# A hybrid attention and convolution layer: a convolution branch is moved beside the attention, its weights are kept in DRAM, and its norm runs in float32r

## The chip, the cores and the metric

The kernel runs on one core of a Trainium2 chip. The metric is the time of one execution on the device in microseconds (us). The time before is the median of three runs, 3138.69 us (3136.90 to 3145.14).

A core has a matrix engine (TensorE, PE in the profile; PEld is its loading of weights), a vector engine (VectorE, DVE), an activation engine (ScalarE, ACT), GpSimd (POOL) and SyncE (SP), which here issues all transfers. Each engine works through its own queue in order and waits for the others by semaphores.

## The reference

One layer over a sequence of 2048 tokens of width 1024, in float32. The input is normalised and projected by one matrix to nine blocks of 1024 columns. One branch is a stick-breaking attention with 16 heads of 64, one a causal convolution of 31 taps for each channel with a layer norm over the channels. Each branch has a gate inside, a projection, and a gate for the sum.

```python
h = x @ w_in
q, k, v, z_sb, c_val, c_gate, z_cv, g_sb, g_cv = jnp.split(h, SPLIT_POINTS, axis=-1)
o_sb = _stick_breaking_attention(to_heads(q), to_heads(k), to_heads(v)).reshape(bsz, seq, SB_WIDTH)
y_sb = (o_sb * jax.nn.silu(z_sb)) @ w_sb_proj
u = c_val * jax.nn.sigmoid(c_gate)
u = _causal_depthwise_conv(u, conv_w, conv_b)          # 31 taps per channel
u = jax.nn.silu(_layer_norm(u, conv_ln_g, conv_ln_b))
y_cv = (u * jax.nn.silu(z_cv)) @ w_cv_proj
merged = jax.nn.sigmoid(g_sb) * y_sb + jax.nn.sigmoid(g_cv) * y_cv
return _layer_norm(DEEPNORM_ALPHA * x + merged @ w_out, ln_g, ln_b)
```

## The kernel before

**Tiling.** Activations lie with channels on the 128 partitions. The sequence is reversed and cut into four chunks c of 512 tokens, and two halves h of 1024: half 1 (chunks 3 and 2) holds the earliest tokens, half 0 (chunks 1 and 0) the later ones. A matrix has eight blocks m of 128 rows. Every float32 product is made of three float32r products: a tensor is cut into a high and a low part by `split` (a copy on ACT, a subtraction on VectorE), and the matrix engine adds high x high, high x low and low x high. A projection block for one chunk is then 24 matmuls of 128x512 in one PSUM bank, in four pieces of six (`Fill.parts`, L201).

**Stages.** 1. First phase: the input projections by a scheme with seven instead of eight block products (L909), half 1 first, then a part of half 0. The convolution goes beside it. 2. Attention: eight pairs of heads for half 1, then for half 0. A head computes scores (`lg`, L583 and L584), a sigmoid on ACT (`nb`, L586), a scan on VectorE (L589), transposes (`tp`, L612), a split into `th` and `tl` (L117), and the products with the values (`pv`, L628). 3. End: what is left of the branches, the output product (`output`, L1243) and the last norm.

**What sets the order.** TensorE's instructions run in the order in which the program issues them. Other work for TensorE during the attention is a list of pieces, `F.pieces`: the k, q, v and z projections of half 0, then the branch projections s (after the attention) and c (after the convolution) of half 1. The list is dealt out over the attention by place: each pair of heads has a stretch of the list (`spans`, with SPLIT for half 1's share), and the list's last END places are left for after the attention. A piece without matmuls counts as a place too. On the other engines a scheduler orders by priority and data.

**The convolution** of a channel block and a half is a generator, `conv_steps`, of some 50 steps, most of them one tap on VectorE (L409). `slow_step` is called after each piece and adds PACES[phase] to a credit; with a credit of 1 or more it does one step:

```python
def slow_step(now=False):
    marks.append(newest())
    pace[0] += PACES[phase[0]]
    if not now and (not slow or pace[0] < 1):
        pace[0] = min(pace[0], 1.0)
        return
    pace[0] -= 1
    ...
        while slow and next(slow[0], slow) is slow:
            slow.pop(0)
```

The inner loop passes over generators that are used up and stops at the first step done. `u` in the first phase is the group that makes the convolution's input for one block.

**The norm of the convolution** goes by items: `conv_mean` sums over channels by a matmul with ones, then `conv_ln` for each chunk subtracts the mean and squares (s2, L467 to L474), sums the squares by matmuls with one column of ones (m2, L483), spreads the factor (m3, L494), and applies norm, gain and gates (s3, L501 to L505). Between them stand empty items, W1 or W0 in number, so that TensorE does not meet a matmul before its data. Items are set among the pieces by F.delay and F.soon (every N1 pieces for half 0).

**Branches.** `branch(n, h)` projects; its eviction multiplies by a gate (L712). The second branch of a half adds the first one's result (`other`, L714). `load_w` loads a weight block of 512 KB and splits it, unless its halves lie in DRAM already (`wdr`; so far only for some blocks of w_in). `loads` brings activations back from DRAM and splits them. Before, half 1 takes s then c beside the attention; in the end stage s of half 0, outputs of chunks 3 and 2, c of half 0, outputs 1 and 0.

**Buffers.** "st" tiles (128x512) are seven, shared by evictions, loads and the norm. mm has two PSUM banks.

Of the kernel before, what the change touches and what calls it, by code (L numbers as in the profile page):

```python
# [8 lines left out]
F32 = mybir.dt.float32  # L9
# [20 lines left out]
LAG = 3  # L30
PACES = [0.78, 1.25, 0.6]
I0 = 1
SPLIT = 0.27
RD = 9
W1 = 5
END = 14
W0 = 3
N1 = 2
O0 = 25
# [15 lines left out]
def layer_kernel(ctx: ExitStack, tc, x, w_in, w_sb, w_cv, w_out, vecs, cw, rows, out):  # L55
# [14 lines left out]
    ones = const.tile([P, P], F32, name="ones")  # L70
    nc.gpsimd.memset(ones, 1.0 / D)
    vec = const.tile([P, 5, KB], F32, name="vec")
    g_in, b_in, c_b, c_g, c_lb = (vec[:, i, :] for i in range(5))
# [70 lines left out]
    def load_w(src, col):  # L144


        hi, lo = (wp.tile([P, KB, P], F32R, name="w4", bufs=4) for _ in range(2))
        for g in range(2):
            ks = slice(g * 4, g * 4 + 4)
            if (id(src), col, g) in wdr:  # L150
                for t, e in ((hi, 0), (lo, 1)):
                    dma(t[:, ks], wdr[id(src), col, g][:, e])
                continue
            raw = wp.tile([P, 4, P], F32, name="wraw", bufs=2)
            nc.sync.dma_start(out=raw, in_=src[col // P][:, ks])
            split(raw, hi[:, ks], lo[:, ks])
        return hi, lo

# [281 lines left out]
    def conv_mean(h):  # L440

        def mean(c):
            while len(convs) < (2 - h) * KB:
                slow_step(True)
            ps, mu, ys = mm_p.tile([P, CH], F32, name="mm"), st(), st()
            dma(ys.rearrange("p (e n) -> p e n", e=2), ysd[h][:, :, c % 2 * 256:c % 2 * 256 + 256])
            nc.tensor.matmul(ps, lhsT=ones, rhs=ys, start=True, stop=True)
            nc.scalar.activation(mu, ps, AF.Copy)
            dma(mud[c], mu)
        return [lambda c=c: mean(c) for c in half(h)]  # L450

    def conv_ln(c):
# [11 lines left out]
        def s2(m):  # L464
# [5 lines left out]
            if m == 0:  # L470
                box["sq"] = sg_p.tile([P, CH], F32, name="sum", bufs=1)
                nc.vector.tensor_copy(out=box["sq"], in_=y)
            else:
                nc.vector.tensor_tensor(out=box["sq"], in0=box["sq"], in1=y, op=ALU.add)  # L474

        def m1():
# [3 lines left out]
        def m2():  # L480
            ps = mm_p.tile([P, CH], F32, name="mm")
            for b in range(nb):
                nc.tensor.matmul(ps[:, b:b + 1], lhsT=box["sq"][:, b * P:(b + 1) * P], rhs=ones[:, 0:1], start=True, stop=True)  # L483
            v = sm.tile([P, nb], F32, name="var", bufs=2)
            nc.vector.tensor_copy(out=v, in_=ps[:, :nb])
            rsqrt_eps(v, v, nb)
            box["v"] = v

        def m3():
            ps = mm_p.tile([P, CH], F32, name="mm")  # L490
            rb = st()
            nc.vector.tensor_copy(out=rb.rearrange("p (b r) -> p b r", b=nb), in_=box["v"].unsqueeze(2).to_broadcast([P, nb, P]))
            for b in range(nb):
                nc.tensor.matmul(ps[:, b * P:(b + 1) * P], lhsT=rb[:, b * P:(b + 1) * P], rhs=ident, start=True, stop=True)  # L494
            box["rs"] = copied(ps)

        def s3(m):
# [10 lines left out]
        wait = [lambda: None] * (W1 if h else W0)  # L508
        return ([m1] + wait + [(lambda m=m: s2(m)) for m in range(KB)] + wait + [m2] + wait + [m3]
                + [(lambda m=m: s3(m)) for m in range(KB)])  # L510
# [182 lines left out]
    def branch(n, h):  # L693

        def gate(m):
            def load(c):
# [20 lines left out]

        src, bys = (w_sb, [gate]) if n == "s" else (w_cv, [gate, other])
        return [(src, m * P, [(c, lambda c=c: acts[n, c]) for c in half(h)], use(m)) + tuple(b(m) for b in bys)
# [21 lines left out]
    def first_phase(F, x2, w1, ps_p):  # L741
# [257 lines left out]
        def order(h):  # L999
            us_ = [("u", m) for m in range(KB)]  # L1000
            rest = [(e, m) for m in range(4) for e in ("kqvzcgh" if h else "cgh")]
            out_ = []
            for n, u in enumerate(us_):
                out_.append(u)
                out_ += rest[len(rest) * n // 8:len(rest) * (n + 1) // 8]
            return out_

# [140 lines left out]
    with ExitStack() as s2:  # L1148
# [9 lines left out]
        for i in range(NPAIR):  # L1158
            ready[1, i] = True
        norm = conv_mean(1) + conv_ln(3) + conv_ln(2)  # L1160
        for i in range(NPAIR):
            fill_qkv(F, 0, i)
            if i < NPAIR - 2:
                F.block(*gate_z(i))
            for q in range(10):
                if norm and i >= I0:
                    F.delay(1 + 3 * q, 0.1, norm.pop(0))
        F.pair(gate_z(NPAIR - 2), gate_z(NPAIR - 1), freed=loads("s", 1))
        F.soon([(0.1, it) for it in norm], 1, 2)
        run(F, branch("s", 1), loads("c", 1))  # L1170
        F.soon([(0.1, it) for it in conv_mean(0) + conv_ln(1) + conv_ln(0)], N0, N1)
        run(F, branch("c", 1), loads("s", 0))
        end = len(F.pieces) - END
# [28 lines left out]
    with ExitStack() as s2:  # L1202
# [74 lines left out]
        run(F, branch("s", 0), loads("m", 1))  # L1277
        output(F, 3, loads("c", 0)[0])
        output(F, 2, loads("c", 0)[1])
        run(F, branch("c", 0), loads("m", 0))  # L1280
        output(F, 1, ())
# [36 lines left out]
```

## Time and profile before

| | us |
|---|---|
| median of three runs | 3138.69 |
| the profiled execution, its own time | 3146.49 |
| its span in the trace | 3144.7 |
| TensorE busy | 2896.8 |
| VectorE busy | 2603.8 |
| ScalarE busy | 1414.0 |
| first score matmul (L583) starts | 1204.0 |
| last product with the values (L628) ends | 2741.3 |

The profile is of one execution. Its numbers are read in three ways here: busy time of each engine in a stretch, with the clock that the throttle granted TensorE; idle time of an engine by what ended it ("PE tp L612 <- DVE nb L589" is the matrix engine that waited at line 612 for a tile that VectorE wrote at line 589; us in total, times, longest); and groups of like instructions. Matmuls are pipelined, so the duration of one is longer than its step from the last.

### The profile page before, as it was taken

What the parts mean: (1) busy time and instruction counts of PE and PEld (TensorE: products, weight loads), DVE (VectorE), ACT (ScalarE), POOL (GpSimd) and SP (SyncE); (2) the same over time, 40 slices, a digit from 0 to 9 for tenths busy, and PEclk for the clock granted to TensorE, in tenths of its full rate; (3) what the DMA queues carried; (4) which work ended last, traced back from release to release, by engine and by line L of the source; (5) the groups of instructions that cost most, each with busy time, mean ns of one, the idle gap of its engine ahead of it and who ended that gap; (6) DMA issues with size and microseconds to landing.
All of it is one profiled execution on the core that took longest, in us unless ns stands there. A gap on an engine that the chain in (4) does not pass through costs nothing.

```text
span 3144.7 us, 42164 instructions
## 1 busy us (share of the span) xinstructions
PE 2896.8 (92%) x14666; PEld 2402.7 (76%) x14666; DVE 2603.8 (83%) x3537; ACT 1414.0 (45%) x2582; POOL 75.4 (2%) x162
## 2 busy tenths in 40 slices
PE   6998999999999998899889889998899888879998
PEld 4776787878788886787777778887788777767887
DVE  8988989888777865998999988888988898856746
ACT  6553444444422323444454554555645555543322
POOL 1000000000000000000000000000000000000000
PEclk8999999999999999999999999999999999989999
DMA  5878757577865567555563454444543553486552
GB/s 179 301 232 307 264 194 267 206 264 282 286 222 185 176 228 218 169 182 176 182 185 119 149 172 134 156 146 140 167 129 118 158 180 120 145 288 231 169 187 81
DMA packets 319269, 604.98 MB, mean 192 GB/s; under 512 B 37456, under 2 KB 79568, under 8 KB 318928
## 3 DMA queue, kind: packets, MB, share of 16 engines
q1 hardware_dynamic: 319056, 602.29, 58.3%
q8 instruction: 115, 1.88, 0.3%
q14 instruction: 98, 0.80, 0.1%
HBM read 355.74 MB, written 246.42 MB: 191 GB/s over the span
## 4 chain that ended last, share of the span: by engine, by line
PE 47%; DVE 25%; issue 12%; DMA 7%; ACT 3%; SPq 1%; POOL 1%; DVEq 0%; POOLq 0%; ACTq 0%
PE pb L909 11%; PE mm L201 10%; DVE nb L589 10%; PE pp L909 7%; PE mm L909 7%; DVE tl L117 4%; PE tp L612 4%; PE pv L628 3%; PE lg L583 1%; DVE cy L409 1%; PE lg L584 1%; ACT th L116 1%; DVE cu L409 1%; ACT nb L586 1%; DMA st<-fdr 1%
## 5 line engine op out<-in xcount | busy, mean ns | idle before, releaser
L116 ACT ACTIVATE th<-tp 128x512 fp32r<-128x512 f32 (+1 forms) x576 | 329.6, 573 | 467.8 <-PE tp L612 459.2
L117 DVE TENSOR_TENSOR tl<-tp,th 128x512 fp32r<-128x512 f32 (+1 forms) x576 | 374.2, 652 | 92.2 <-ACT th L116 89.1
L612 PE MATMUL tp<-ident,nb 128*128 128x128 f32 x2176 | 354.6, 279 | 80.4 <-DVE nb L589 63.5
L586 ACT ACTIVATE nb<-lg 128x512 f32<-128x512 f32 (+3 forms) x640 | 331.3, 532 | 115.7 <-PE lg L584 114.0
L589 DVE TENSOR_TENSOR_SCAN nb<-nb,dd 128x256 f32<-128x256 f32 (+7 forms) x256 | 343.8, 1348 | 18.0 <-ACT nb L586 18.0
L628 PE MATMUL pv<-tl,v 128*128 128x256 f32 (+1 forms) x1152 | 303.1, 292 | 53.2 <-DVE tl L117 52.5
L612 PEld LDWEIGHTS tp<-ident,nb 128*128 128x128 f32 x2176 | 255.2, 142 | 116.7 <-DVE nb L589 78.8
L589 DVE TENSOR_TENSOR_SCAN nb<-nb,zero 128x1024 f32<-128x1024 f32 x128 | 300.1, 2347 | 23.3 <-ACT nb L586 23.1
L628 PE MATMUL pv<-th,v 128*128 128x256 f32 (+1 forms) x1152 | 307.8, 285 | 2.8 <-ACT th L116 2.6
L583 PE MATMUL lg<-k,qd 128*128 128x512 f32 (+3 forms) x640 | 267.9, 420 | 23.7 <-ACT nb L586 11.7
L628 PEld LDWEIGHTS pv<-tl,v 128*128 128x128 f32 x1152 | 219.1, 190 | 91.7 <-DVE tl L117 76.4
L628 PEld LDWEIGHTS pv<-th,v 128*128 128x128 f32 x1152 | 219.7, 191 | 20.5 <-ACT th L116 4.5
L584 PE MATMUL lg<-k,ql 128*128 128x512 f32 (+3 forms) x640 | 234.7, 367 | 0.0
L201 PE MATMUL mm<-A11h,w 128*128 128x512 f32 x512 | 185.6, 409 | 12.7 <-ACT w L116 7.0
L409 DVE SCALAR_TENSOR_TENSOR cy<-cu,csum,cy 128x512 f32<-128x512 f32 x240 | 179.2, 747 | 18.9 <-ACT cy L405 15.8
L201 PE MATMUL mm<-A12h,w 128*128 128x512 f32 x512 | 188.0, 413 | 0.0
L201 PE MATMUL mm<-SXh,w 128*128 128x512 f32 x512 | 182.8, 403 | 2.1 <-DVE st L712 2.1
L201 PE MATMUL mm<-A22h,w 128*128 128x512 f32 x512 | 182.7, 403 | 0.0
L409 DVE SCALAR_TENSOR_TENSOR cu<-cd,cwt,cu 128x512 f32<-128x512 f32 x240 | 179.1, 746 | 3.7
L409 DVE SCALAR_TENSOR_TENSOR cy<-cu,cwt,cy 128x512 f32<-128x512 f32 x240 | 179.1, 746 | 2.6
L583 PEld LDWEIGHTS lg<-k,qd 128*128 128x128 f32 x640 | 122.5, 191 | 48.7 <-ACT nb L586 29.0
L584 PEld LDWEIGHTS lg<-k,ql 128*128 128x128 f32 x640 | 123.7, 193 | 8.8 <-issue 0.2
(251 smaller groups left out, 6298.9 us busy)
## 6 DMA issues: line engine op xcount, KB each, us to landing
wdr<-w4x SPq DMA_DIRECT2D x78, 512.0 KB, 3.4
wdr<-w SPq DMA_DIRECT2D x68, 512.0 KB, 3.2
w4x<-wdr SPq DMA_DIRECT2D x52, 512.0 KB, 4.7
wraw<-in_w_in SPq DMA_DIRECT2D x100, 256.0 KB, 3.5
w<-wdr SPq DMA_DIRECT2D x96, 256.0 KB, 3.8
k<-kdr SPq DMA_DIRECT2D x192, 128.0 KB, 3.0
v<-vdr SPq DMA_DIRECT2D x96, 256.0 KB, 3.0
w<-wdr SPq DMA_DIRECT2D x46, 512.0 KB, 4.4
```

The lines of the kernel that those rows point to most:

```text
L116: nc.scalar.activation(hi, src, AF.Copy)
L117: nc.vector.tensor_tensor(out=lo, in0=src, in1=hi.bitcast(F32), op=ALU.subtract)
L201: nc.tensor.matmul(box["ps"], lhsT=l[:, kb], rhs=r[kb], start=(kb == 0 and n == 0), stop=(kb == KB - 1 and n == 2))
L409: nc.vector.scalar_tensor_tensor(out=dst, in0=src[:, j:j + HN], scalar=t, in1=first, op0=ALU.mult, op1=ALU.add)
L583: nc.tensor.matmul(lg[:, :w], lhsT=qd[c][:, js], rhs=k2[kc][:, ko:ko + w], start=True, stop=False)
L584: nc.tensor.matmul(lg[:, :w], lhsT=ql[c][:, js], rhs=k2[kc][:, ko:ko + w], start=False, stop=True)
L586: nc.scalar.activation(nb[:, o:o + w], lg[:, :w], AF.Sigmoid, scale=-QS)
L589: nc.vector.tensor_tensor_scan(out=nb[:, :w], data0=nb[:, :w], data1=dd[:, :w] if diag else zero.to_broadcast([P, w]), initial=0.0 if diag ...
L612: nc.tensor.transpose(out=tp[:, at_:at_ + P], in_=tiles[j][:, so:so + P], identity=ident)
L628: nc.tensor.matmul(o[:, :w], lhsT=lv, rhs=tt[:, o0:o0 + w], start=(diag and t == 0 and n == 0 and e == 0), stop=(last and t == nt - 1 and ...
L909: nc.tensor.matmul(bank, lhsT=wt[:, e, kb], rhs=xs_[kb][a], start=start and kb == 0 and n == 0, stop=kb == 3 and n == 2, skip_group_check= ...
```

## The change

1. The pace of the convolution in the second part of the first phase goes from 1.25 to 1.6, and the order of groups has the u groups earlier.
2. Branch c of half 0 moves from the end stage into the list beside the attention, behind branch c of half 1. It is then the first branch of its half, so s of half 0 adds its result. The norm of half 0 begins before branch s of half 1, with an item at every piece instead of every second (N1). END is 20 instead of 14.
3. `load_w` writes the split halves of w_sb and w_cv to DRAM when they are made for half 1 and reads them for half 0.
4. The norm's sums run on float32r halves (`onesr`), with two empty-item spacings changed, and the spreading of the factor is a transpose.

```diff
-PACES = [0.78, 1.25, 0.6]
+PACES = [0.78, 1.6, 0.6]
-END = 14
+END = 20
-N1 = 2
+N1 = 1
...
+    onesr = const.tile([P, P], F32R, name="onesr")
+    nc.scalar.activation(onesr, ones, AF.Copy)
...
             split(raw, hi[:, ks], lo[:, ks])
+            if src is not w_in:
+                d = wdr[id(src), col, g] = dram([P, 2, 4, P], F32R, f"wdr{len(wdr)}b")
+                dma(d[:, 0], hi[:, ks])
+                dma(d[:, 1], lo[:, ks])
...
-        def mean(c):
+        parts = {}
+
+        def prepare():
             while len(convs) < (2 - h) * KB:
                 slow_step(True)
-            ps, mu, ys = mm_p.tile([P, CH], F32, name="mm"), st(), st()
-            dma(ys.rearrange("p (e n) -> p e n", e=2), ysd[h][:, :, c % 2 * 256:c % 2 * 256 + 256])
-            nc.tensor.matmul(ps, lhsT=ones, rhs=ys, start=True, stop=True)
+            for c in half(h):
+                ys = st()
+                dma(ys.rearrange("p (e n) -> p e n", e=2), ysd[h][:, :, c % 2 * 256:c % 2 * 256 + 256])
+                parts[c] = st(F32R), st(F32R)
+                split(ys, *(t if len(ys.shape) == 2 else t.rearrange("p (e n) -> p e n", e=2) for t in parts[c]))
+
+        def mean(c):
+            ps, mu = mm_p.tile([P, CH], F32, name="mm"), st()
+            for n, t in enumerate(parts.pop(c)):
+                nc.tensor.matmul(ps, lhsT=onesr, rhs=t, start=n == 0, stop=n == 1)
...
-        return [lambda c=c: mean(c) for c in half(h)]
+        return [prepare] + [lambda: None] * W1 + [lambda c=c: mean(c) for c in half(h)]
...
+            if m == KB - 1:
+                box["sp"] = st(F32R), st(F32R)
+                split(box["sq"], *box["sp"])
...
-                nc.tensor.matmul(ps[:, b:b + 1], lhsT=box["sq"][:, b * P:(b + 1) * P], rhs=ones[:, 0:1], start=True, stop=True)
+                for n, t in enumerate(box["sp"]):
+                    nc.tensor.matmul(ps[:, 2 * b:2 * b + 2], lhsT=t[:, b * P:(b + 1) * P], rhs=onesr[:, 0:2], start=n == 0, stop=n == 1)
...
-        src, bys = (w_sb, [gate]) if n == "s" else (w_cv, [gate, other])
+        src, bys = w_sb if n == "s" else w_cv, [gate] if n == "sc"[h == 0] else [gate, other]
...
+            n = 3 if h else 1
             out_ = []
-            for n, u in enumerate(us_):
-                out_.append(u)
-                out_ += rest[len(rest) * n // 8:len(rest) * (n + 1) // 8]
-            return out_
+            for m in range(KB):
+                out_ += [("u", m)] + rest[m * n:m * n + n]
+            return out_ + rest[KB * n:]
...
-        F.soon([(0.1, it) for it in norm], 1, 2)
+        F.soon([(0.1, it) for it in slots], 1, 2)
+        F.soon([(0.1, it) for it in conv_mean(0) + conv_ln(1) + conv_ln(0)], N0, N1)
         run(F, branch("s", 1), loads("c", 1))
-        F.soon([(0.1, it) for it in conv_mean(0) + conv_ln(1) + conv_ln(0)], N0, N1)
-        run(F, branch("c", 1), loads("s", 0))
+        run(F, branch("c", 1), loads("c", 0))
+        run(F, branch("c", 0), loads("s", 0))
...
         run(F, branch("s", 0), loads("m", 1))
-        output(F, 3, loads("c", 0)[0])
-        output(F, 2, loads("c", 0)[1])
-        run(F, branch("c", 0), loads("m", 0))
+        output(F, 3, loads("m", 0)[0])
+        output(F, 2, loads("m", 0)[1])
```

The built programs show the order on each engine. Line numbers of the changed kernel are higher: L604 is its score matmul, L610 its scan, L633 its transpose, L649 its product with the values, L207 its projection matmul, L415 its tap, L119 the subtraction of a split, L734 the eviction by a gate and L736 the addition of the other branch.

VectorE where the attention begins, before: taps (`cy<-cu,cwt,cy`), evictions of the first phase (L757), then the first scans (`nb<-nb,dd`).

```order
L409 SCALAR_TENSOR_TENSOR cy<-cu,cwt,cy 128x512 x8
L757 TENSOR_TENSOR st<-pp,st 128x512
L409 SCALAR_TENSOR_TENSOR cy<-cu,cwt,cy 128x512
L432 TENSOR_TENSOR ys<-ys,cu 128x512
L409 SCALAR_TENSOR_TENSOR cy<-cu,cwt,cy 128x512
L757 TENSOR_TENSOR gt<-pb,gt 128x512
L409 SCALAR_TENSOR_TENSOR cy<-cu,cwt,cy 128x512 x2
L518 COPY dd<-ident 128x128
L117 TENSOR_TENSOR SXl<-st,SXh 128x512 x4
L589 SCALAR_TENSOR_TENSOR nb<-nb,dd 128x256
```

The same place in the changed kernel.

```order
L415 SCALAR_TENSOR_TENSOR cy<-cu,cwt,cy 128x512 x8
L779 TENSOR_TENSOR st<-pp,st 128x512
L415 SCALAR_TENSOR_TENSOR cy<-cu,cwt,cy 128x512
L438 TENSOR_TENSOR ys<-ys,cu 128x512
L415 SCALAR_TENSOR_TENSOR cy<-cu,cwt,cy 128x512
L779 TENSOR_TENSOR gt<-pb,gt 128x512
L415 SCALAR_TENSOR_TENSOR cy<-cu,cwt,cy 128x512 x2
L539 COPY dd<-ident 128x128
L119 TENSOR_TENSOR SXl<-st,SXh 128x512 x4
L610 SCALAR_TENSOR_TENSOR nb<-nb,dd 128x256
```

Nothing moved here: the rows are the same, and 598 taps of 736 stand ahead of the first scan in both (13 of 16 channel blocks).

TensorE late in the attention, behind 530 of the 640 score matmuls, before: transposes (`tp`), products with the values (`pv`), and a piece of six projection matmuls (`mm<-A11h,w`).

```order
L612 MATMUL tp<-ident,nb 128x128 x4
L628 MATMUL pv<-th,v_23366 128x256
L628 MATMUL pv<-tl,v_23366 128x256
L628 MATMUL pv<-th,v_23366 128x256
L628 MATMUL pv<-tl,v_23366 128x256
L612 MATMUL tp<-ident,nb 128x128 x4
L201 MATMUL mm<-A11h,w_23967 128x512
L201 MATMUL mm<-A11l,w_23967 128x512
L201 MATMUL mm<-A11h,w_23968 128x512
L201 MATMUL mm<-A11h,w_23967 128x512
L201 MATMUL mm<-A11l,w_23967 128x512
L201 MATMUL mm<-A11h,w_23968 128x512
```

The same place in the changed kernel.

```order
L633 MATMUL tp<-ident,nb 128x128 x4
L207 MATMUL mm<-A11h,w_24643 128x512
L207 MATMUL mm<-A11l,w_24643 128x512
L207 MATMUL mm<-A11h,w_24644 128x512
L207 MATMUL mm<-A11h,w_24643 128x512
L207 MATMUL mm<-A11l,w_24643 128x512
L207 MATMUL mm<-A11h,w_24644 128x512
L649 MATMUL pv<-th,v_23930 128x256
L649 MATMUL pv<-tl,v_23930 128x256
L649 MATMUL pv<-th,v_23930 128x256
L649 MATMUL pv<-tl,v_23930 128x256
L633 MATMUL tp<-ident,nb 128x128 x4
```

A piece now stands behind nearly every group of transposes here; before, most groups had only the products behind them. Between the 520th and the 560th score matmul stand 252 projection matmuls instead of 114; over the sixteen stretches of 40 the counts were 156, 156, 138, 138, 132, 144, 150, 150, 144, 144, 96, 174, 168, 114, 132, 138 and are 180, 192, 144, 150, 156, 162, 180, 156, 168, 114, 120, 126, 108, 252, 162, 258.

VectorE just behind the attention, before: splits of loaded activations (`SXl`, `A22l`), of w_out (`wol`) and of w_sb (`w<-wraw,w`), and the norm of the last chunk (`st<-st,mu` and `sum`).

```order
L467 TENSOR_TENSOR st<-st,mu 128x512
L117 TENSOR_TENSOR SXl<-st,SXh 128x512 x2
L117 TENSOR_TENSOR wol<-raw,woh 128x1024
L467 TENSOR_TENSOR st<-st,mu 128x512
L117 TENSOR_TENSOR wol<-raw,woh 128x1024
L472 COPY sum<-st 128x512
L117 TENSOR_TENSOR SXl<-st,SXh 128x512
L117 TENSOR_TENSOR A22l<-st,A22h 128x512
L117 TENSOR_TENSOR w_27171<-wraw,w_27170 128x512
L474 TENSOR_TENSOR sum<-sum,st 128x512
L712 TENSOR_TENSOR st<-mm,gt 128x512
```

The same place in the changed kernel.

```order
L119 TENSOR_TENSOR wol<-raw,woh 128x1024
L119 TENSOR_TENSOR A12l<-st,A12h 128x512 x2
L119 TENSOR_TENSOR wol<-raw,woh 128x1024
L734 TENSOR_TENSOR st<-mm,gt 128x512
L119 TENSOR_TENSOR SXl<-st,SXh 128x512 x4
L119 TENSOR_TENSOR A22l<-st,A22h 128x512
L734 TENSOR_TENSOR st<-mm,gt 128x512
L736 TENSOR_TENSOR st<-st 128x512
L119 TENSOR_TENSOR A22l<-st,A22h 128x512 x3
```

The norm and the splits of w_sb are gone from behind the attention; the norm stands ahead of the last scan now.

More of the change, by code (lines that the diff above doesn't have):

```diff
@@ L482, in m2 @@
             for b in range(nb):
-                nc.tensor.matmul(ps[:, b:b + 1], lhsT=box["sq"][:, b * P:(b + 1) * P], rhs=ones[:, 0:1], start=True, stop=True)
+                for n, t in enumerate(box["sp"]):
+                    nc.tensor.matmul(ps[:, 2 * b:2 * b + 2], lhsT=t[:, b * P:(b + 1) * P], rhs=onesr[:, 0:2], start=n == 0, stop=n == 1)
             v = sm.tile([P, nb], F32, name="var", bufs=2)
-            nc.vector.tensor_copy(out=v, in_=ps[:, :nb])
+            nc.vector.tensor_copy(out=v, in_=ps[:, :2 * nb].rearrange("p (b e) -> p b e", e=2)[:, :, 0])
             rsqrt_eps(v, v, nb)
@@ L489, in m3, with m4 @@
         def m3():
-            ps = mm_p.tile([P, CH], F32, name="mm")
-            rb = st()
+            box["rb"] = rb = st()
             nc.vector.tensor_copy(out=rb.rearrange("p (b r) -> p b r", b=nb), in_=box["v"].unsqueeze(2).to_broadcast([P, nb, P]))
+        def m4():
+            ps, rb = mm_p.tile([P, CH], F32, name="mm"), box["rb"]
             for b in range(nb):
-                nc.tensor.matmul(ps[:, b * P:(b + 1) * P], lhsT=rb[:, b * P:(b + 1) * P], rhs=ident, start=True, stop=True)
+                nc.tensor.transpose(out=ps[:, b * P:(b + 1) * P], in_=rb[:, b * P:(b + 1) * P], identity=ident)
             box["rs"] = copied(ps)
@@ L508, in conv_ln @@
         wait = [lambda: None] * (W1 if h else W0)
-        return ([m1] + wait + [(lambda m=m: s2(m)) for m in range(KB)] + wait + [m2] + wait + [m3]
+        return ([m1] + wait + [(lambda m=m: s2(m)) for m in range(KB)] + wait + [m2] + wait[1:] + [m3, lambda: None, m4]
                 + [(lambda m=m: s3(m)) for m in range(KB)])
@@ L999, in order @@
         def order(h):
-            us_ = [("u", m) for m in range(KB)]
             rest = [(e, m) for m in range(4) for e in ("kqvzcgh" if h else "cgh")]
+            n = 3 if h else 1
             out_ = []
-            for n, u in enumerate(us_):
-                out_.append(u)
-                out_ += rest[len(rest) * n // 8:len(rest) * (n + 1) // 8]
-            return out_
+            for m in range(KB):
+                out_ += [("u", m)] + rest[m * n:m * n + n]
+            return out_ + rest[KB * n:]
         groups = [group(1, *o) for o in order(1)] + [group(0, *o) for o in order(0)]
@@ L1160, in layer_kernel @@
         norm = conv_mean(1) + conv_ln(3) + conv_ln(2)
+        slots = [lambda: norm.pop(0)() for _ in norm]
         for i in range(NPAIR):
@@ L1164, in layer_kernel @@
                 F.block(*gate_z(i))
-            for q in range(10):
-                if norm and i >= I0:
-                    F.delay(1 + 3 * q, 0.1, norm.pop(0))
+            for q in range(13):
+                if slots and i >= I0:
+                    F.delay(1 + 2 * q, 0.1, slots.pop(0))
         F.pair(gate_z(NPAIR - 2), gate_z(NPAIR - 1), freed=loads("s", 1))
-        F.soon([(0.1, it) for it in norm], 1, 2)
+        F.soon([(0.1, it) for it in slots], 1, 2)
+        F.soon([(0.1, it) for it in conv_mean(0) + conv_ln(1) + conv_ln(0)], N0, N1)
         run(F, branch("s", 1), loads("c", 1))
-        F.soon([(0.1, it) for it in conv_mean(0) + conv_ln(1) + conv_ln(0)], N0, N1)
-        run(F, branch("c", 1), loads("s", 0))
+        run(F, branch("c", 1), loads("c", 0))
+        run(F, branch("c", 0), loads("s", 0))
         end = len(F.pieces) - END
```

## The prediction, on record before the changed kernel ran

> **What bounds the kernel now.** I read the page's shares and slices first, then the windows of each stage, then who waits for whom, and last the rows of single groups.
>
> ```profile
> PE 2896.8 (92%) x14666; PEld 2402.7 (76%) x14666; DVE 2603.8 (83%) x3537; ACT 1414.0 (45%) x2582; POOL 75.4 (2%) x162
> PE   6998999999999998899889889998899888879998
> DVE  8988989888777865998999988888988898856746
> PEclk8999999999999999999999999999999999989999
> DMA  5878757577865567555563454444543553486552
> ```
>
> TensorE is at eight to nine tenths nearly everywhere, so what a move is worth depends on what the rest of that stage does. The stages are cut at the first score matmul (L583), the last product with the values (L628) and the end of the slow stretch behind it. The columns are length, then busy time and count of PE, PEld, DVE, ACT, POOL, then granted clock, DMA share, GB/s.
>
> ```profile
> 0.00:1204.00 1204.00, 1135.66 (x4930) 917.61 (x4931) 999.97 (x1558) 488.17 (x865) 40.87 (x87) 0.98 0.70 239
> 1204.00:2052.40 848.40, 769.23 (x4501) 656.04 (x4501) 754.73 (x923) 428.38 (x846) 13.50 (x22) 0.98 0.54 166
> 2052.40:2434.20 381.80, 351.07 (x2093) 300.03 (x2092) 322.68 (x359) 207.00 (x392) 2.10 (x4) 1.00 0.44 138
> 2434.20:2741.30 307.10, 267.65 (x1567) 227.04 (x1566) 271.05 (x310) 163.22 (x306) 1.02 (x1) 0.97 0.47 148
> 2741.30:2861.00 119.70, 99.12 (x397) 79.67 (x396) 71.19 (x104) 48.27 (x67) 1.01 (x1) 0.89 0.83 275
> 2861.00:3144.70 283.70, 274.03 (x1187) 222.34 (x1185) 184.18 (x285) 78.94 (x108) 16.90 (x47) 0.99 0.47 156
> ```
>
> The reader should see three regimes. The first phase is bound by TensorE. In the attention (1204 to 2741, 1537 us) TensorE is busy for 1388 us and VectorE for 1348: two engines, both near 90%, that wait for each other. In the end stage (403 us) TensorE is the bound, but its first 120 us lose time at a clock of 0.89 and a DMA share of 0.83. Who waits in the attention, and then in the end stage:
>
> ```profile
> PE tp L612 <- DVE nb L589: 63.5, 58, 4.4
> PE pv L628 <- DVE tl L117: 52.5, 77, 2.6
> PE tp L612 <- DVE tl L117: 16.3, 14, 2.2
> PE lg L583 <- ACT nb L586: 11.7, 29, 2.6
> ```
>
> ```profile
> PE mm L201 <- DVE st L712: 7.8, 2, 5.7
> PE mm L201 <- ACT w L116: 7.0, 2, 6.2
> PE mm L483 <- DVE sum L474: 5.8, 1, 5.8
> ```
>
> So the attention holds about 150 us of TensorE idle time, mostly for VectorE's scans and splits, and the change puts matmuls there.
>
> **The convolution in the first phase: 0 us (-10 to +10).** In the order of VectorE 598 of the 736 taps stand ahead of the first scan, before and after, with the same rows around it. The reason is in the code: one call of slow_step does at most one step, and a pace of 1.25 gives one at every piece already; 1.6 only heaps up credit. The title's first part therefore moves nothing out of the attention. The groups of the first phase change places but not number; its row above (94% of 1204 us) leaves 68 us of idle time that could move either way by some.
>
> **The branch c of half 0 leaves the end stage.** By the order, L201 matmuls behind the last L628 fall from 798 to 444: 354 fewer. Their price, where nothing waits, is a row with TensorE full:
>
> ```profile
> 3000.00:3100.00 100.00, 100.00 (x436) 81.53 (x435) 58.18 (x89) 24.21 (x34) 4.19 (x12) 1.00 0.46 153
> ```
>
> 100 us / 436 = 0.229 us, so -354 x 0.229 = -81 us. The stretch 2741 to 2861 holds 397 matmuls worth 91 us and took 120: 29 us lost. The three waits above are 21 us of it; the clock lost the rest:
>
> ```profile
> 2790.00:2800.00 10.00, 10.00 (x34) 8.15 (x34) 5.21 (x7) 3.81 (x4) 1.01 (x1) 0.68 0.90 333
> 2830.00:2840.00 10.00, 7.76 (x25) 6.03 (x26) 6.99 (x10) 4.20 (x6) 0.00 (x0) 0.80 0.92 292
> ```
>
> All three waits lie on work that goes away here. The sum L474 belongs to the norm of the last chunk, which now ends beside the attention; the w of L116 is a split of w_sb, whose halves now come from DRAM (32 pairs of splits gone from ACT and DVE here); the L712 eviction stood on VectorE behind norm steps and splits. I take -21 of 29 and leave 8. The bounds are -5 (the loads become the next wait, below) and -29. End stage: -102 us (-86 to -110).
>
> By the Trainium skill (TensorE: Matmul & The Clock Gate, "HAM oscillation — how this bites in real kernels"), an idle gap longer than the activity window of about 3.4 us throttles the clock, at a cost of its own. The clocks 0.68 and 0.80 behind the gaps agree. Were it alone to set the loss, all 29 us would go with the gaps, and the end stage would give -110; the sum keeps -102.
>
> **The same 354 matmuls enter the attention: +81 us of TensorE work.** What that costs is read from stretches of equal attention work. I cut the attention at every 40th L583 matmul; these are the last six of the sixteen pieces. By the order they hold 96, 174, 168, 114, 132 and 138 L201 matmuls.
>
> ```profile
> 2146.80:2242.80 96.00, 80.07 (x480) 67.47 (x479) 88.07 (x104) 60.51 (x114) 0.00 (x0) 0.98 0.49 156
> 2242.80:2343.30 100.50, 94.64 (x563) 81.12 (x562) 86.88 (x98) 51.63 (x96) 0.00 (x0) 1.00 0.48 151
> 2343.30:2434.20 90.90, 88.61 (x525) 76.23 (x524) 73.05 (x77) 46.65 (x89) 0.00 (x0) 1.00 0.38 118
> 2434.20:2530.80 96.60, 84.71 (x501) 71.08 (x499) 86.00 (x98) 53.38 (x103) 0.00 (x0) 0.98 0.54 162
> 2530.80:2627.20 96.40, 85.88 (x510) 73.65 (x511) 86.09 (x99) 48.44 (x92) 1.02 (x1) 0.98 0.49 152
> 2627.20:2741.30 114.10, 97.06 (x560) 82.31 (x559) 98.95 (x115) 61.40 (x112) 0.00 (x0) 0.96 0.40 134
> ```
>
> With VectorE at 86 to 88 us, pieces with 96, 114, 132 and 174 of them take 96.0, 96.6, 96.4 and 100.5 us: 78 more (17.9 us) cost 4.5, a quarter, while VectorE is the slower. With little VectorE work (third row) the time is TensorE's 88.6 plus 2.3: there each costs in full. VectorE's own price is about 0.7 (second to third row: 13.8 less DVE and 1.4 less fill, 9.6 less time).
>
> VectorE gets 78 more instructions between the first and last scan (1585 to 1663): 40 of the norm of the last chunk, 16 evictions (L712), 11 splits of activations, 8 new splits for the float32r norm, some small ones. Back to back such an instruction takes 0.61 us, start to start:
>
> ```profile
> 2742.65 0.69 DVE L712 TENSOR_TENSOR st<-mm,gt 128x512 f32<-128x512 f32 x1
> 2743.26 0.68 DVE L117 TENSOR_TENSOR w<-wraw,w 128x512 fp32r<-128x512 f32 x1
> ```
>
> That is about 48 us, and ACT gets 44 more, which its share (428 of 848, 207 of 382) hides. In place, by the order:
> - 1204 to 2052: +180 L201 (41 us), VectorE about +27. A quarter of the one and 0.7 of the other give 29; pieces here with 85 us on both engines need more, so +36.
> - 2052 to 2434: the norm now has an item at every piece (N1 = 1), so matmuls fall by 114 (-26 us) and VectorE rises by about 40, to 363 of 382 us. It is the bound there: 0.7 x 40 = 28, less what TensorE gives back at 0.5, +15: I take +12.
> - 2434 to 2741: +288 L201 (66 us), VectorE -19. Two of the three pieces get 252 and 258 and become TensorE's: by the third row's rule, work plus some 5%, 307 becomes about 333: +26.
>
> Sum +74. The low end is +45 (a quarter of 81 plus half of 48), the high end 81 + 0.7 x 48 = +115.
>
> **The norm by float32r.** The mean's four fp32 matmuls leave two records each; eight at 0.59 us against eight of 0.229. Their waits are rows of two sums:
>
> ```profile
> L447 PE MATMUL mm<-st,ones x8: 590/591/592, 1433.0 to 2492.2; 128*128 128x512 f32 x8
>   DVE sum L474: 12.1, 2
> ```
>
> At most -3 us on the matmuls; of the 12.1 the 5.8 in the end stage are counted already, and the other 6.3 may stay, since m2 now also waits for a split. Against it, prepare holds four of the seven "st" tiles, and sp two, for some pieces, so evictions and loads can find none. Taken: +1 (-6 to +15).
>
> **Queues.** SP issues 176 more DMAs in the attention (1111 to 1287) and 80 fewer behind it; a store of a weight half waits for its split, and loads of k and v stand behind it. SP waits there already in long sums:
>
> ```profile
> SPq L93 <- PE lg L584: 130.4, 88, 9.0
> SPq L93 <- DVE og L649: 118.2, 30, 12.9
> ```
>
> The first are loads that wait for tiles that TensorE still reads: SP runs ahead of it, and that lead is the cover. If it is spent, each late load stops L583 for some us; this is in the +15. POOL has 167 instructions in both.
>
> **Sum.** 0 - 102 + 74 + 1 = -27 us on a span of 3144.7 (its run: 3146.5), so about 3118. The median of the runs is 3138.7, 7.8 below the profiled run; against it, 3112.
>
> **The rivals.**
> - The attention hides more: only the low +45. For it speak the rows where 78 matmuls cost 4.5 us; against it that two late pieces are filled beyond their VectorE time. 45 - 102 + 1 = -56: 3083.
> - No change: s0 is held by its loads. A block of branch s takes 48 x 0.229 = 11 us; in it would move 1 MB of weight halves (0.5 before), four 256 KB loads, two stores, and w_out: near 300 GB/s, and the stretch before shows 333 at most, at a DMA share of 0.90. If the waits stay (-86) and the attention pays 80, the sum is -5: 3134. Against it: some 10 MB of norm traffic leave this stretch. The Trainium skill (DMA: Bandwidth & Descriptors, "Where 436 GB/s comes from") puts the ceiling at 358 to 435 GB/s, by which there is room; no run here shows such a rate.
> - Slower: the attention pays in full. The fill is dealt out by places in a list, and norm items take places; so VectorE limits the middle, TensorE the late pieces, and neither fills the other's gaps. +115 - 102 + 1 = +14: 3153. It decides from +110 in the attention; the third row, where TensorE's time is the piece's time, speaks for it, the flat four pieces against.
>
> **How the numbers follow.** A run of this kernel tells about 0.3% (9 us) from no change; the three shown span 8 us. Chances: forecast 0.47, hides more 0.20, no change 0.18, slower 0.15. The first two are faster (0.67). The range of the likeliest alone is 3098 to 3128, its attention between +60 and +90. Over all cases the range goes from 3075, a little below the second case, since its terms can add up too (-102 may be -110), to 3150, just short of the slower case; that leaves out under 1 in 10 below and a little over 1 in 10 above.
>
> **What would show it.** Right: the first score matmul starts near 1204 us again with 13 of 16 channel blocks convolved; the last L628 product near 2815; about 300 us behind it, with no wait of L483 or of w for a split; in the attention the slices of the last fifth with TensorE at 9 and VectorE lower, those ahead of it with VectorE at 9. Wrong: a later first phase; a last fifth in which TensorE still waits 10% (the mechanism of the fill); L201 waiting for DMA on w in the end stage (the second rival); L583 waiting for k or v (the queue).

## The result and the profile after

| | before | after |
|---|---|---|
| median, us | 3141.91 (3136.90 to 3145.40, 4 runs) | 3102.43 (3098.92 to 3109.97, 4 runs) |
| ratio | | 0.9879, 95% interval 0.9853 to 0.9904 |
| span of the profiled execution, us | 3144.7 | 3108.2 |

The kernel is 1.2% faster, 39 us by the medians and 36.5 by the two spans. The forecast was 27, with a range of 3075 to 3150 that holds the 3102. Stages are read from one execution each, and the profiled one of the change (3110.0 us) is 7.5 above its median, so differences of a few us between the stages of two traces are not told apart by them. First the page's shares and slices after the change.

```profile
PE 2880.1 (93%) x14650; PEld 2396.0 (77%) x14650; DVE 2588.4 (83%) x3513; ACT 1402.1 (45%) x2559; POOL 76.4 (2%) x162
PE   6998999999999998899989899989888899999998
DVE  8998889888778775999998887788898988764586
PEclk8999999999999999999999999999999999999999
```

The busy time of TensorE has hardly moved (2896.8 us before); it is packed more densely at the end. The same stages as before, cut at the same score matmuls (first of all, after 360, after 520), at the last product with the values and at the end:

```profile
0.00:1198.30 1198.30, 1129.48 (x4930) 913.15 (x4931) 1000.69 (x1558) 488.53 (x866) 40.79 (x87) 0.98 0.70 241
1198.30:2088.10 889.80, 808.35 (x4701) 693.01 (x4702) 782.98 (x972) 454.46 (x885) 16.35 (x26) 0.98 0.56 175
2088.10:2481.40 393.30, 340.56 (x1979) 288.31 (x1978) 358.75 (x423) 229.92 (x429) 2.03 (x2) 0.97 0.61 195
2481.40:2807.50 326.10, 317.25 (x1833) 272.73 (x1832) 255.01 (x277) 146.47 (x273) 0.00 (x0) 0.99 0.51 165
2807.50:3108.20 300.70, 284.42 (x1212) 228.80 (x1211) 191.02 (x285) 82.77 (x106) 17.27 (x47) 0.98 0.55 186
```

| stage | before | after | difference | forecast |
|---|---|---|---|---|
| first phase | 1204.0 | 1198.3 | -5.7 | 0 |
| attention, first 360 score matmuls | 848.4 | 889.8 | +41.4 | +36 |
| next 160 | 381.8 | 393.3 | +11.5 | +12 |
| last 120 | 307.1 | 326.1 | +19.0 | +26 |
| end stage | 403.4 | 300.7 | -102.7 | -102 |

So the sums came out nearly as forecast, and the late stretch reads as expected: TensorE busy for 317 of 326 us, VectorE for 255. The waits of TensorE in the attention, and then in the end stage:

```profile
PE tp L633 <- DVE nb L610: 69.4, 57, 3.3
PE pv L649 <- DVE tl L119: 35.5, 50, 2.0
PE lg L604 <- ACT nb L607: 14.9, 27, 2.6
PE tp L633 <- DVE tl L119: 13.9, 15, 2.9
```

```profile
PE mm L207 <- DMA w<-wdr50b: 3.7, 1, 3.7
PE mm L207 <- DMA w<-wdr62b: 2.3, 1, 2.3
PE mm L207 <- DMA w<-wdr48b: 0.6, 1, 0.6
```

The reader should see two things. In the attention TensorE is idle about as long in sum as before (149 us before, 143 now), although it is busy for 78 us more. In the end stage the waits for the norm, the eviction and the split are gone, and in their place TensorE waits for the halves of w_sb from DRAM. That the sums fit does not show that each part did what was said. The runs take the parts apart.

### The profile page after: what moved, and what is told of

It reads as the page before. It is cut to its first block, busy times and chain, and to the rows that moved or that the text cites. A ratio compares the mean times of both kernels' runs of the same rounds, so it can differ in the third digit from the quotient of the medians.

```text
span 3108.2 us, 42166 instructions
## 1 busy us (share of the span) xinstructions
PE 2880.1 (93%) x14650; PEld 2396.0 (77%) x14650; DVE 2588.4 (83%) x3513; ACT 1402.1 (45%) x2559; POOL 76.4 (2%) x162
## 4 chain that ended last, share of the span: by engine, by line
PE 55%; DVE 21%; issue 9%; DMA 6%; ACT 3%; SPq 1%; POOL 1%; DVEq 0%; POOLq 0%; ACTq 0%
PE mm L207 14%; PE pb L931 12%; PE mm L931 8%; DVE nb L610 8%; PE pp L931 8%; PE tp L633 4%; PE pv L649 4%; DVE tl L119 4%; PE lg L604 2%; PE lg L605 2%; DVE cy L415 1%; SPq L95 1%; ACT th L118 1%; ACT nb L607 1%; PE mo L1266 1%
## 5 line engine op out<-in xcount | busy, mean ns | idle before, releaser
L119 DVE TENSOR_TENSOR tl<-tp,th 128x512 fp32r<-128x512 f32 (+1 forms) x576 | 373.2, 651 | 106.4 <-ACT th L118 103.8
L633 PE MATMUL tp<-ident,nb 128*128 128x128 f32 x2176 | 356.7, 280 | 84.5 <-DVE nb L610 69.4
L610 DVE TENSOR_TENSOR_SCAN nb<-nb,dd 128x256 f32<-128x256 f32 (+7 forms) x256 | 343.5, 1347 | 21.8 <-ACT nb L607 21.6
L633 PEld LDWEIGHTS tp<-ident,nb 128*128 128x128 f32 x2176 | 254.8, 143 | 118.7 <-DVE nb L610 85.5
L649 PE MATMUL pv<-tl,v 128*128 128x256 f32 (+1 forms) x1152 | 301.5, 290 | 36.5 <-DVE tl L119 35.5
L610 DVE TENSOR_TENSOR_SCAN nb<-nb,zero 128x1024 f32<-128x1024 f32 x128 | 299.7, 2346 | 30.6 <-ACT nb L607 30.3
L649 PE MATMUL pv<-th,v 128*128 128x256 f32 (+1 forms) x1152 | 305.9, 284 | 0.7 <-ACT th L118 0.7
L604 PE MATMUL lg<-k,qd 128*128 128x512 f32 (+3 forms) x640 | 264.4, 414 | 25.7 <-ACT nb L607 14.9
L649 PEld LDWEIGHTS pv<-tl,v 128*128 128x128 f32 x1152 | 220.4, 191 | 70.2 <-DVE tl L119 54.7
L649 PEld LDWEIGHTS pv<-th,v 128*128 128x128 f32 x1152 | 220.6, 191 | 17.3 <-ACT th L118 1.4
L415 DVE SCALAR_TENSOR_TENSOR cy<-cu,csum,cy 128x512 f32<-128x512 f32 x240 | 178.9, 745 | 20.9 <-ACT cy L411 17.6
L207 PE MATMUL mm<-A11h,w 128*128 128x512 f32 x512 | 186.4, 407 | 6.6 <-DMA w<-wdr50b 3.7
L207 PE MATMUL mm<-A12h,w 128*128 128x512 f32 x512 | 189.4, 414 | 0.0
L207 PE MATMUL mm<-SXh,w 128*128 128x512 f32 x512 | 184.9, 405 | 0.0
L207 PE MATMUL mm<-A22h,w 128*128 128x512 f32 x512 | 184.0, 403 | 0.0
L415 DVE SCALAR_TENSOR_TENSOR cu<-cd,cwt,cu 128x512 f32<-128x512 f32 x240 | 178.7, 745 | 3.3
L415 DVE SCALAR_TENSOR_TENSOR cy<-cu,cwt,cy 128x512 f32<-128x512 f32 x240 | 178.9, 745 | 2.9
L604 PEld LDWEIGHTS lg<-k,qd 128*128 128x128 f32 x640 | 123.1, 192 | 50.2 <-ACT nb L607 28.4
```

The source lines that it names most:

```text
L119: nc.vector.tensor_tensor(out=lo, in0=src, in1=hi.bitcast(F32), op=ALU.subtract)
L207: nc.tensor.matmul(box["ps"], lhsT=l[:, kb], rhs=r[kb], start=(kb == 0 and n == 0), stop=(kb == KB - 1 and n == 2))
L415: nc.vector.scalar_tensor_tensor(out=dst, in0=src[:, j:j + HN], scalar=t, in1=first, op0=ALU.mult, op1=ALU.add)
L604: nc.tensor.matmul(lg[:, :w], lhsT=qd[c][:, js], rhs=k2[kc][:, ko:ko + w], start=True, stop=False)
L610: nc.vector.tensor_tensor_scan(out=nb[:, :w], data0=nb[:, :w], data1=dd[:, :w] if diag else zero.to_broadcast([P, w]), initial=0.0 if diag ...
L633: nc.tensor.transpose(out=tp[:, at_:at_ + P], in_=tiles[j][:, so:so + P], identity=ident)
```

## Experiments: the parts one by one

Ratios are to the kernel before on the same chip; 0.001 is 3.1 us. Intervals reach 0.0011 to 0.0026 to either side.

| kernel | median, us | ratio (95% interval) |
|---|---|---|
| the change | 3102.4 | 0.9879 (0.9853 to 0.9904) |
| first phase alone | 3142.7 | 0.9998 (0.9987 to 1.0009) |
| move alone | 3118.7 | 0.9921 (0.9908 to 0.9935) |
| change without weights in DRAM | 3095.4 | 0.9848 (0.9832 to 0.9864) |
| change with the old norm | 3126.8 | 0.9944 (0.9929 to 0.9958) |
| change with w_cv alone in DRAM | 3099.4 | 0.9849 (0.9834 to 0.9863) |

**First phase alone**: the kernel before with the new pace and the new order of groups.

```diff
-PACES = [0.78, 1.25, 0.6]
+PACES = [0.78, 1.6, 0.6]
...
+            n = 3 if h else 1
+            for m in range(KB):
+                out_ += [("u", m)] + rest[m * n:m * n + n]
+            return out_ + rest[KB * n:]
```

> The kernel before with the first part of the change alone: the pace 1.6 and the new order of the groups in the first phase. My theory: the pace does nothing (one step at a piece either way), and the order of the groups is worth what the trace after shows, the first score matmul at 1198 instead of 1204 us: ratio to before 0.998 (3136 us), taps ahead of the first scan 598. Rival: the 6 us are the difference of two executions, ratio 1.000. The title's reading, convolution really moved: 3100 or less.

Ratio 0.9998: the rival holds. The first score matmul starts at 1199.4 us in this run's trace, but with the same first phase it starts anywhere up to 1206.8 (with w_cv alone in DRAM, below), so the 1198 us is the spread of executions. (The pace alone changes nothing by construction: the changed kernel with 1.25 in place of 1.6 builds to the same program.)

**Move alone**: branch c of half 0 beside the attention with N1 = 1, END = 20 and the earlier norm of half 0, on the kernel before.

```diff
-END = 14
+END = 20
-N1 = 2
+N1 = 1
...
-        run(F, branch("c", 1), loads("s", 0))
+        run(F, branch("c", 1), loads("c", 0))
+        run(F, branch("c", 0), loads("s", 0))
...
-        run(F, branch("c", 0), loads("m", 0))
```

> The kernel before with the move of branch c of half 0 alone (with the earlier norm of half 0, N1 = 1 and END = 20); weights split anew, norm in fp32, first phase as before. My theory: the move carries nearly all of it: the end stage loses 81 us of matmuls and the waits of the norm, but keeps splits of w_sb (about 8 us of the 103 stay), the attention grows by about 72: near 3113 us, ratio 0.991. Rival: the weights in DRAM free the end stage, and without them the move alone is worth under 10 us: 3132 or more.

0.9921, 25 us: most of the change, though a little less than the 0.991 that I expected; the rival (under 10 us) is out. Its attention and its end stage:

```profile
1203.30:2825.30 1622.00, 1471.34 (x8525) 1259.07 (x8526) 1402.44 (x1678) 837.47 (x1595) 19.68 (x28) 0.97 0.51 164
2825.30:3114.90 289.60, 279.93 (x1213) 227.20 (x1211) 200.26 (x301) 92.33 (x122) 17.28 (x47) 0.99 0.52 176
```

The end stage takes 289.6 us with no wait for any weight, 11 us less than in the full change, although it splits w_sb anew. The three waits of before are gone by the move alone. The attention takes 1622, 85 more than before and 13 more than the full change.

**Without the weight halves in DRAM**: the full change with these lines taken out.

```diff
-            if src is not w_in:
-                d = wdr[id(src), col, g] = dram([P, 2, 4, P], F32R, f"wdr{len(wdr)}b")
-                dma(d[:, 0], hi[:, ks])
-                dma(d[:, 1], lo[:, ks])
```

> The changed kernel without the halves of w_sb and w_cv in DRAM: they are split each time. My theory: 32 pairs of splits come back, those of branch c beside the attention (16 x 0.61 us on a VectorE that limits part of it) and those of branch s in the end stage, where w waited 7 us: +8 to +14 us on the changed kernel, near 3113. Rival: the 24 MB of added traffic and SP's longer queue cost as much as they save: 3102, no difference.

Both were wrong: it is faster than the change, 0.9848 against 0.9879 (10 us by the ratios). The stretch of 120 us behind the attention, in the change and then without the halves in DRAM:

```profile
2807.50:2927.00 119.50, 112.90 (x478) 91.19 (x478) 55.16 (x76) 28.69 (x39) 0.00 (x0) 0.97 0.89 301
```

```profile
2804.10:2923.60 119.50, 119.50 (x526) 98.48 (x526) 73.13 (x107) 43.46 (x62) 1.05 (x3) 1.00 0.83 282
```

In the same time TensorE gets through 526 matmuls instead of 478, at the full clock, though VectorE and ACT do 31 and 23 instructions more. In the change a block brings 1 MB of halves in this stretch, where otherwise 0.5 MB is read and split. Its loss stands in two places, behind the waits of 3.7 us for wdr50b and 2.3 us for wdr62b shown above: after each, the granted clock is 0.50 for 3.4 us (2831.1 to 2834.5 and 2902.7 to 2906.1 in the trace of the change). The 6.6 us of waits (0.6 for wdr48b among them) and 2 x 1.7 us lost to the clock make the 10 us. Loads of halves in that stretch, issue to landing in the last column; 3.8 us was the median of such loads before:

```profile
w<-wdr50b SPq DMA_DIRECT2D x2, 256.0 KB, 5.6
w<-wdr56b SPq DMA_DIRECT2D x2, 256.0 KB, 8.2
w<-wdr57b SPq DMA_DIRECT2D x2, 256.0 KB, 8.4
```

The slowest loads are not the ones that cost: for wdr56b and wdr57b TensorE never waited. What counts is whether a block lands before its first matmul.

**w_cv alone in DRAM** tells whether the cost is this reading or the writing beside the attention.

```diff
-            if src is not w_in:
+            if src is w_cv:
```

> The changed kernel with the halves of w_cv alone in DRAM, w_sb split each time (none in DRAM: 3095, both: 3102). My theory: the 7 us are the waits for w in the end stage, which reads w_sb, so w_cv in DRAM costs nothing: 3093 to 3096. Rival: the stores and SP's queue cost beside the attention, where both weights are written: about half, 3098 or more.

0.9849, the same as none (0.9848). By the median, 3099, the rival would hold, but the kernel before was slower too in that series (3147); the ratio decides. Its end stage shows no wait for w. So w_cv in DRAM costs and saves nothing that can be measured. What remains is w_sb, and the waits and the slow clock in the end stage account for its 10 us; w_sb alone in DRAM was not run.

**The old norm** in the full change: conv_mean and conv_ln as before, fp32 and old places.

```diff
-        return [prepare] + [lambda: None] * W1 + [lambda c=c: mean(c) for c in half(h)]
+        return [lambda c=c: mean(c) for c in half(h)]
...
-[m2] + wait[1:] + [m3, lambda: None, m4]
+[m2] + wait + [m3]
```

> The changed kernel with the norm's sums in fp32 as before, and the old places of its items. My theory: at most 3 us of matmuls and some waits come back, 8 splits and the held tiles go: 3100 to 3107. Rival one: the held st tiles cost, so fp32 is faster by 5 us or more. Rival two: the early preparation of the mean matters, so fp32 is slower by 10 us or more.

0.9944 against 0.9879: 20 us slower: the second rival, at twice the 10 us that it gave as the least. The same difference stands between the move alone (0.9921) and the change without halves in DRAM (0.9848), 23 us, whose attention takes 1599.6:

```profile
1204.50:2804.10 1599.60, 1457.43 (x8509) 1247.61 (x8510) 1404.42 (x1686) 839.29 (x1603) 19.23 (x28) 0.98 0.52 166
```

TensorE's work is much the same (1457 and 1471 us) and so is VectorE's; what differs is 8 us of idle time and 14 of busy time, in which the mean clock is 0.97 instead of 0.98 and 16 more matmul records stand.

## Experiments: format or places

The base from here is the change without halves in DRAM (0.9848). **fp32 in the new places**: sums in fp32 without splits, the load for the mean in the item prepare, all empty items as in the change, and the spreading (by matmuls again) in its new place.

```diff
-                parts[c] = st(F32R), st(F32R)
-                split(ys, *(t if len(ys.shape) == 2 else t.rearrange("p (e n) -> p e n", e=2) for t in parts[c]))
+                ys = parts[c] = st()
...
-            if m == KB - 1:
-                box["sp"] = st(F32R), st(F32R)
-                split(box["sq"], *box["sp"])
```

> The base with the norm's sums in fp32 and no splits for them, but with the early loading for the mean, the new empty items and the spreading two items behind its copy. The move alone (old norm) took 3119, the base 3095: 23 us lie in the norm. My theory: TensorE's waits at the mean and at the spreading (each about 4 us with a slow clock behind it) are what the new norm saves, and the places of its items do that: 3095 to 3102. Rival: fp32 on TensorE costs by itself, and the places save little: 3112 or more.

3090.3, 0.9838 (0.9823 to 0.9853): not slower than float32r, and no difference that the intervals could tell. So the format is worth nothing that can be measured here; the places hold the whole 26 us against the move alone (0.9921). Its attention has as many instructions on TensorE and VectorE as that of the move alone, which took 1622 us with TensorE busy for 1471:

```profile
1204.20:2802.80 1598.60, 1462.83 (x8525) 1253.39 (x8526) 1399.90 (x1678) 837.55 (x1595) 19.71 (x28) 0.98 0.52 166
```

**The mean's load put back** into the item of its matmul, and apart from it **the spreading's copy put back** into the item of its matmuls:

```diff
-            for c in half(h):
-                ys = parts[c] = st()
-                dma(ys.rearrange("p (e n) -> p e n", e=2), ysd[h][:, :, c % 2 * 256:c % 2 * 256 + 256])
 
         def mean(c):
+            ys = parts[c] = st()
+            dma(ys.rearrange("p (e n) -> p e n", e=2), ysd[h][:, :, c % 2 * 256:c % 2 * 256 + 256])
             ps, mu = mm_p.tile([P, CH], F32, name="mm"), st()
```

> The fp32 norm in its new places (3090) with the other thing put back: the sum over channels is loaded in the item that also holds its matmul, so that TensorE can wait for the load, twice for each half. My theory: one wait of about 4 us or none: 3091 to 3098. Rival as above: 3090. If this and the run of the spreading give back less than half of the 28 us between the move alone (3119) and 3090, the places of the items are the larger part.

```diff
-[m2] + wait[1:] + [m3, lambda: None, m4]
+[m2] + wait[1:] + [lambda: None, lambda: None, lambda: (m3(), m4())]
```

> The fp32 norm in its new places (3090) with one thing put back: the copy that spreads the factor stands in the same item as the four matmuls that read it, so that TensorE waits there for VectorE. All items keep their places. My theory: each of the four spreadings can cost TensorE up to 4 us and a slow clock behind it: 3096 to 3104. Rival: the shift of all later items by some places is what the new norm gains, and this wait is nothing: 3090.

The mean's load without its lead gives 0.9874 against 0.9838, 11 us. TensorE waits for it in the trace, here of the kernel with that load put back:

```profile
PE mm L454 <- DMA st<-ysd: 12.0, 3, 5.5
```

The spreading costs nothing (0.9835). So in the new places the load's lead is worth 11 us. That does not make it 11 of the 26, for with the old norm the same load is waited for much less. The move alone, then the kernel with fp32 in the new places (where no wait for ysd or at the spreading is left):

```profile
PE tp L612 <- DVE nb L589: 75.5, 56, 5.0
PE mm L447 <- DMA st<-ysd: 4.4, 2, 3.9
PE mm L494 <- DVE st L492: 3.9, 1, 3.9
```

```profile
PE tp L622 <- DVE nb L599: 64.0, 55, 3.3
```

The norm's own waits are 8 us of it; the waits of the transposes for the scans are 11.5 us longer in the move alone. That points at the shift of the items, and of the pieces between them, against the attention, more than at items that meet their data late. No run took that apart, and it stays open.

## Experiments: what a matmul costs beside the attention

**Pieces dealt by matmuls**: the base with the list dealt out by its pieces with matmuls instead of by all its places, so that the stretches of 40 score matmuls hold 138 to 186 instead of 108 to 258 of them.

```diff
+        cum = [0]
+        for c_, _ in F.pieces:
+            cum.append(cum[-1] + (1 if c_ > 1 else 0))
...
-            at_fill = max(at_fill, lo + int((hi - lo) * k / work[p_]))
+            at_fill = max(at_fill, place(int(lo + (hi - lo) * k / work[p_])))
```

> The changed kernel without weight halves in DRAM (3095 us, called the base from here), with the pieces dealt out over the attention by their matmuls and not by places in the list: the sixteen stretches hold 138 to 186 projection matmuls, where the base has 108 to 258. My theory: the stretches with 252 and 258 are TensorE's and those with 108 to 126 VectorE's, so levelling saves about 17 us in the attention: near 3078. Rival: a matmul costs TensorE its time wherever it stands (the slope over all stretches), and levelling gives nothing: 3095.

0.9856 against 0.9848: no difference, and the rival holds. Middle and late stretch, first of the base, then of the levelled kernel:

```profile
2087.80:2475.10 387.30, 335.79 (x1979) 285.01 (x1978) 358.55 (x423) 230.01 (x429) 2.02 (x2) 0.97 0.54 171
2475.10:2804.10 329.00, 318.03 (x1833) 272.71 (x1832) 263.31 (x293) 154.70 (x289) 0.00 (x0) 0.99 0.41 133
```

```profile
2062.90:2490.40 427.50, 384.95 (x2203) 327.24 (x2202) 382.99 (x462) 244.41 (x451) 4.53 (x5) 0.97 0.58 184
2490.40:2795.30 304.90, 288.27 (x1689) 246.25 (x1688) 249.48 (x273) 150.24 (x282) 0.00 (x0) 0.99 0.38 123
```

The middle gets 224 more records (some 50 us of TensorE) and takes 40 us longer; the late stretch loses 144 (33 us) and gains 24. A microsecond of matmuls costs about 0.7 to 0.8 in either, whether VectorE is at 359 of 387 us or at 263 of 329. This price holds what moves along with the pieces: VectorE has 24 us more work in the middle and 14 less late. The first 360 score matmuls, which give up the other 80 records (18 us) and 14 us of VectorE, take 863.5 instead of 883.3 us: no cheaper, and rather the full price.

**Steps by full credit**: the base with a slow_step that does what the pace says.

```diff
-        pace[0] -= 1
-        with ...
-            while slow and next(slow[0], slow) is slow:
-                slow.pop(0)
+        n_ = 1 if now else int(pace[0])
+        pace[0] -= n_
+        for _ in range(n_):
+            with ...
+                while slow and next(slow[0], slow) is slow:
+                    slow.pop(0)
```

> The base with a slow_step that does as many steps as its credit allows, so that the pace 1.6 takes effect: 690 of 736 taps stand ahead of the first scan, 598 in the base. My theory: VectorE has room in the second part of the first phase (58 to 77% busy there), the attention loses 102 VectorE instructions (about 65 us) in its first six stretches, whose TensorE work leaves some 36 us to gain, less about 10 in the first phase: near 3070. Rival: the taps delay evictions in the first phase, which then pays what the attention gains: 3095.

3080.0, 0.9806: 13 us better than the base, half of what I expected. First phase and attention:

```profile
0.00:1202.40 1202.40, 1133.78 (x4931) 916.32 (x4931) 1068.46 (x1660) 490.09 (x868) 41.48 (x87) 0.98 0.69 241
1202.40:2786.40 1584.00, 1457.46 (x8509) 1250.73 (x8510) 1342.70 (x1584) 837.82 (x1601) 17.10 (x28) 0.98 0.52 167
```

The first phase takes 67 us more of VectorE work at no cost. The attention loses 62 us of it and is 15.6 us shorter: a quarter for each, where I had put 0.7. The work left the first six stretches of 40 score matmuls; what VectorE's work costs later was not measured.

**Both**: the last two edits together.

> The base with both: pieces dealt by matmuls, and the convolution's steps by full credit. My theory: the two act in different stretches and add up: near 3053. Rival: with the convolution gone the first stretches have room that levelling takes fill away from, so the sum is 10 us or more short of that: 3063 or more.

3069.1, 0.9771 (0.9758 to 0.9785): 24 us better than the base, and the best kernel here; 38 of the 72 us against the kernel before are the change's own. The rival holds (3063 or more). Levelling, worth nothing by itself, gives 11 us once the convolution is out of the early stretches. My theory had 42.

**For speed**: both, with the fp32 norm in its new places and another share.

```diff
-SPLIT = 0.27
+SPLIT = 0.29
```

> A version for speed: the fp32 norm in its new places, no weight halves in DRAM, convolution by full credit, pieces dealt by matmuls, and 0.29 instead of 0.27 of the fill in the first half, whose VectorE work is lighter now. The version with both and the float32r norm took 3069; fewer splits give some 3 us, the new share some 3: near 3063. Rival: the share was right at 0.27 and the fp32 norm no faster: 3069 or more.

3102.5, 0.9856: 27 us slower than both, where the rival had said 3069 or more. The loss is in the attention; its worst stretch of 40 score matmuls, then the same stretch of the kernel with both:

```profile
2285.20:2414.00 128.80, 107.29 (x570) 89.17 (x569) 109.80 (x138) 68.84 (x125) 1.01 (x1) 0.91 0.65 201
```

```profile
2263.20:2373.60 110.40, 100.50 (x574) 86.02 (x572) 103.84 (x132) 66.35 (x121) 1.01 (x1) 0.95 0.69 218
```

With as many matmuls it takes 18 us more. Share and norm were changed together, so which of them it is stays open.

## Why the prediction was right, point by point

- **First phase, 0 us**: right. The pace does nothing, the order of groups nothing (0.9998).
- **End stage, -102**: -102.7, by a wrong route. I counted the split of w_sb among the waits that the DRAM halves take away, and took -21 of the 29 us lost there. The move alone takes all three waits away (289.6 us, -114: 81 of matmuls and 33 of waits and clock). The halves bring 11 us back, as loads that land late and the slow clock behind them. This is the mechanism of the second rival, at a smaller size: I had it as a bound and left it out of the sum.
- **Attention, +74**: +71.9. The work that I put in is in the trace: TensorE is busy for 78 us more, VectorE for 48. The price of a quarter per microsecond of matmuls, read from four stretches with equal VectorE work, was wrong: levelling shows 0.7 to 0.8. Those stretches also differed in which norm items they held. And VectorE's price is a quarter (steps by full credit, early stretches), not 0.7. The two errors cancelled, which is luck. With the new prices 0.75 x 81 + 0.25 x 48 = 73, but that is a fit made afterwards and no test: the move alone, with the same matmuls, grew by 85.
- **The late stretch, +26**: +19, with a slip in my sum. Work plus 5% of 268 + 66 us is 350, which is +43; the 333 that I wrote is the bare work. It came out near only because TensorE's busy time there grew by 50 us (268 to 317) and not by 66; the time is that work plus 3%.
- **The norm, +1 (-6 to +15)**: this is the step that failed. It measured -20 to -26 us, outside its bounds. I priced the format and the waits that stood in the trace before, and not the places of the items. In the move alone, with the norm in its old places, the attention grew by 85 us; with the new places by 72. My terms for the attention and the norm missed both, and the misses partly cancelled.
- **The sum, -27**: about -39 by the medians. By the ratios the move is worth 25 us, the new places of the norm some 23, and the halves of w_sb take 10 back. So the direction and the main step, the move, were right, and the closeness of the three stage sums was in part luck.
- **Held st tiles, longer SP queue**: nothing of them shows. L604 never waits long for k or v after its first (10.7 us; 11.1 before), and w_cv's halves, written and read beside the attention, cost nothing.
- **The clock rule**: the Trainium skill (TensorE: Matmul & The Clock Gate, "HAM oscillation — how this bites in real kernels") would have let all 29 us go with the gaps. The traces agree: without halves in DRAM no gap is left, the clock is 1.00 and 526 records fill 119.5 us. But the rule's window of about 3.4 us is no safe bound: in the change a gap of 2.3 us was followed by a clock of 0.50, too.
- **Rivals**: the slower one, attention in full at +115, was refuted at +72; the better one at +45 too. No change was refuted by the 39 us, though its late loads of w came.

## What to carry to other kernels

Where two engines wait for each other at 90% each, take the price of added work from a run that moves that work, and look at what moves with it; stretches of one trace differ in more than the count that is read. A result kept in memory to save two engines with room can cost more than it saves when it is read where TensorE has no cover. And a load set some items ahead of the matmul that reads it was worth 11 us, not far from half of what moving the branch gave. Check in the built order, too, that a parameter can act at all: the pace could not.

## What was not expected of the hardware

With no gap behind the attention, TensorE ran 119.5 us at a granted clock of 1.00, one matmul of 128x512 every 0.227 us, while the DMA share was 0.83 at 282 GB/s (without halves in DRAM). In the change, at 0.89 and 301 GB/s, single loads of 256 KB took 8.2 and 8.4 us to land, more than twice the median of 3.8, and cost nothing, because their blocks were needed later. Two waits of 2.3 and 3.7 us cost some 1.7 us more each than they lasted: behind either the granted clock was 0.50 for 3.4 us.
